# One Strassen step moved from the first output unit to the first b unit, two more places for sums, and a root formed from known parts

## The chip, the cores and the metric

The kernel runs on one core of a Trainium2 chip. The metric is the device time of one execution in microseconds (us). Engines are named as in the profile: PE is TensorE's matmul, PEld its weight load, DVE is VectorE, ACT is ScalarE, POOL is GpSimd, SP is SyncE, which issues most weight loads.

## What is computed

One hybrid decoder block over 256 tokens of width 4096, in float32:

```python
h = rmsnorm(x, norm_w)
proj = h @ w_in                            # 4096 x 20480
u_p, z_p, u_c, b_c, c_c, z_c, g_logit = split(proj)
y_pool = causal_multiscale_pool(u_p, pool_w, pool_scale) * silu(z_p)
y_conv = causal_gated_shortconv(u_c, b_c, c_c, conv_w, conv_b) * silu(z_c)
br = einsum('bsnc,ncd->bsnd', stack([y_pool, y_conv]), w_branch)
gates = sigmoid(g_logit.reshape(b, s, 2, d) + gate_b)
x = x + (sum(gates * br, axis=2) @ w_out)
return rmsnorm(x, final_norm_w)
```

Almost all of the work is the three products with w_in, w_branch and w_out.

## The kernel before

**Units and steps.** The products are cut into units of 1024 output columns, in this order: cz0, cb0, cu0, cc0 (convolution, first half), cz1 to cc1, pz0 to pu1 (pool), g0_0 to g1_0 (gates), b0_0, b1_0, ... b1_3 (branches), o0 to o3 (output). A unit over 4096 rows has 16 steps of 256 rows, a branch unit 8. float32 is kept by splitting each operand into a rounded high part and a rest, so every product takes three matmuls. A step is of one of two kinds, given by a letter of the unit's string (lines 38 to 51): P, plain, with 24 matmuls of 128x512, or S, one Strassen step, with 21. The strings' names count the S steps: NINE_A is cb0's, SEVEN4 is o0's, TEN that of cu0 and of the other units with ten.

**What a step asks of the engines.** SP loads the four weight blocks of a step into `raw` (three and a corner); for an S step POOL adds the third block onto the corner with an accumulating DMA (`gather`). ACT rounds them into the ring (`highs`), DVE subtracts to get the rests (`lows`). For an S step DVE also forms three block sums in `parts`, which ACT rounds and DVE splits again (`rest`, line 308). The ring has 26 cells of 128x512: a P step takes 8, an S step 14, and a cell comes free when PE has used it. So the preparation runs one or two steps ahead of PE, never further. All engines run their queues in program order.

**Stationary operands.** They stand in `arena` as high parts and rests. An S operand has, beside its four blocks, four sums of them (Q3, Q5, Q6, Q7, `sums_s`). There is room for eight S operands; a unit with nine or ten uses operands 6 and 7 as well, whose sums share one tile, `side`: `side_items` (line 553) makes them during cb0 and stores both to DRAM (`aside`, on POOL), and later units load the one they need.

**Ticks.** After every six matmuls one entry of a queue is run (`tick`): epilogues are lists of such entries, with None as a pause. `pop_fill` runs beside them: a `Fill` brings one operand of the branch and output units from DRAM, in phases. It is fetched into a stage (three of them: half of `sa`, and `sb`, `sc`); from 8 ticks on, phase 0 forms the four sums on DVE, phase 1 rounds on ACT 4 ticks later, phase 2 makes the rest on DVE. The sums had one place, `sa[:, 0:4]`, so only one S fill could be between its phases 0 and 2 (line 824). The operands of o0's last steps come from the last branch unit, so they are filled while o0 runs.

**The start and the end.** WARM matmuls on zeros run before the first weights land (line 922). In o3 the last three steps are run per token block, the second one also per half; `finish_half` adds a half and squares it, and `finish` forms 1 / sqrt(mean + eps) with one Newton step (`rstd_of`, line 925), scales the four column blocks and stores them.

Of the kernel before, what the change touches and what calls it, by code (L numbers as in the profile page):

```python
# [9 lines left out]
F32 = mybir.dt.float32  # L10
# [5 lines left out]
P = 128  # L16
# [16 lines left out]
WARM = 18  # L33
# [6 lines left out]
NINE_A = "PSPSSPSPSSPSPSPS"  # L40
NINE_P = "PSPSSPSPSSPSSPSP"
HOST = "PPBPPMMPSSSPSSSPSSS"
SEVEN4 = "PPPPSPSPSPSPSSPS"
# [11 lines left out]
def hybrid_block(ctx: ExitStack, tc: tile.TileContext, x, xc, prm, rows_in, w_in, pool_w, w_branch, w_out, out):  # L55
# [5 lines left out]
    def act(dst, src, func=AF.Copy, **kw):  # L61
        return pin(nc.scalar.activation(dst, src, func, **kw))  # L62
# [22 lines left out]
    def move(dst, src):  # L85
        return pin(nc.scalar.dma_start(dst, src))
# [48 lines left out]
    def norm_col(j):  # L135
        return par[:, j:j + 1]
# [391 lines left out]
    def seq_x(text):  # L528
        if text is FIRST:
            return [("P", i) for i in FIRST]  # L530
        text = [c for c in text if c in "PS"]
        ns = text.count("S")
        if ns > NS + NB:
            ss = list(range(ND, 16)) + [resident[0]]
            if ns > NS + NB + 1:
                resident[0] = 2 * ND - 3 - resident[0]
                ss = [ss[-1]] + ss[:-1] + [resident[0]]
            ps = [i for i in range(ND) if i not in ss]
            return [(c, (ss if c == "S" else ps).pop(0)) for c in text]
        return sequence(text, ND, ND + NS + NB, NB)  # L540
# [12 lines left out]
    def side_items(i):  # L553
        def scaled():
            for k in range(2):
                v = sa[:, 6 - 2 * k:8 - 2 * k]
                act(v, v, scale=norm_col(2 * i + k))

        return [lambda: move(sa[:, 4:].rearrange("p o c -> p (o c)"), xc[i])] + gap(7) + [scaled, None, lambda: sums_s(sa)] + gap(3) + [
            lambda: act(side["tile"][:, 0], sa[:, 0:4]), None,  # L560
            lambda: sub(side["tile"][:, 1], sa[:, 0:4], side["tile"][:, 0].bitcast(F32)),
            None, None, None, None, lambda: aside(side_d[i - ND + 2], side["tile"])]
# [10 lines left out]
    def conv_units(c, first):  # L573
# [39 lines left out]
        u = in_unit(f"cz{c}", base + 3 * HALF, lambda u: silu_y(u.late) + (gap(4) + side_items(ND - 1) + side_items(ND - 2) if first else []),  # L613
                    FIRST if first else EIGHT4, dst=Y)
        u.late = not first
        in_unit(f"cb{c}", base + HALF, b_epi, TEN if c else NINE_A).late = True
# [157 lines left out]
    def out_unit(c):  # L774
# [15 lines left out]
        text = (SEVEN4, NINE, NINE, OUT3)[c]  # L790
# [19 lines left out]
    class Fill:  # L810
        def __init__(self, o, src, free, ready):
            self.o, self.free, self.ready, self.src = o, free, ready, src
            self.at = self.st = None
            self.phase = self.due = 0

# [4 lines left out]
        def advance(self, force):  # L820
            o, q = self.o, self.st
            n = o.n - 4 if o.kind == "S" else 0
            four = sa[:, 0:4]
            if self.phase == 0 and n and any(f.phase and f.o.kind == "S" for f in fills):
                return False
# [26 lines left out]
    stages = [sa[:, 4:8]]  # L852
# [315 lines left out]
    for u in units:  # L1168
        if u.name == "b0_0":
            last_pair["stack"].close()  # L1170
            open_last(F32)
        if u is names["o1"]:
            assert not fills
            more.close()
# [13 lines left out]
        if u is last_x:  # L1188
            side["stack"].close()
            more = ExitStack()  # L1190
            ctx.enter_context(more)
            pool = more.enter_context(tc.tile_pool(name="more", bufs=1))
            apart["tile"] = pool.tile([P, 8 * P], F32R, name="apart")
            stages.extend(pool.tile([P, 4, P], F32, name=name) for name in ("sb", "sc"))
            queue_fills()
# [54 lines left out]

    def finish(t):
        r = rout[:, t:t + 1]
        rstd_of(ossq[:, t:t + 1], r, f"rout{t}")
# [9 lines left out]
    for t in range(2):  # L1263
        for ns in ((0, 1),) if t == 0 else ((0,), (1,)):
# [6 lines left out]
            for n in ns:  # L1271
                finish_half(t, n)
        finish(t)
# [40 lines left out]
```

## Time and profile before

| | us |
|---|---|
| median of 3 runs | 2348.76 (2348.66 to 2349.11) |
| the profiled execution | 2348.53 |
| its span in the trace | 2346.8 |
| PE busy | 2332.0 (99%) |
| DVE busy | 2134.0 (91%) |
| ACT busy | 1539.8 (66%) |

The span runs from the first instruction to the last event; the execution takes 1.7 us more. Busy times overlap between engines. A wait in the trace is idle time of an engine just before an instruction, put down to whatever released it last.

### The profile page before, as it was taken

How to read it: one execution, taken by the hardware profiler on the slowest of the kernel's cores; microseconds unless marked ns; L12 is line 12 of the kernel's file. 1: busy time of each engine (PE TensorE's matmuls, PEld its weight loads, DVE VectorE, ACT ScalarE, POOL GpSimd, SP SyncE). 2: the span in 40 equal slices, each digit the busy share in tenths (PEclk: the TensorE clock that was granted, in tenths of full speed). 3: DMA queues.
4: the chain of work that ended last, by engine and by line, in shares of the span. 5: the costliest groups of instructions: out<-in, count | busy, mean ns of one | idle time of the engine just before them, and what ended most of it. 6: DMA issues, size and time to landing. Idle time of an engine off the chain costs nothing.

```text
span 2346.8 us, 29867 instructions
## 1 busy us (share of the span) xinstructions
PE 2332.0 (99%) x10382; PEld 1930.1 (82%) x10382; DVE 2134.0 (91%) x2177; ACT 1539.8 (66%) x1926; POOL 298.7 (13%) x362
## 2 busy tenths in 40 slices
PE   9999999999999999999999999999999999999998
PEld 7888888888888888888888888888888888878886
DVE  8789999999989979979999899998999889999898
ACT  6666656666666656667766766666676667666664
POOL 0111101111101101101121111111011010011110
PEclk9999999999999999999999999999999999999999
DMA  9789978989978868868999999999889889889998
GB/s 376 247 250 291 273 229 248 282 246 284 271 219 256 264 201 252 257 205 255 290 275 276 307 284 284 278 309 288 277 271 279 273 266 295 272 237 303 290 268 288
DMA packets 203975, 634.60 MB, mean 270 GB/s; under 512 B 21424, under 2 KB 29872, under 8 KB 201008
## 3 DMA queue, kind: packets, MB, share of 16 engines
q1 hardware_dynamic: 134912, 485.42, 59.0%
q0 software_dynamic: 51264, 105.40, 24.7%
q10 hardware_dynamic: 17648, 41.87, 4.9%
q8 instruction: 81, 1.33, 0.2%
q14 instruction: 70, 0.57, 0.1%
HBM read 585.42 MB, written 25.17 MB: 260 GB/s over the span
## 4 chain that ended last, share of the span: by engine, by line
PE 95%; DVE 3%; ACT 1%; issue 1%; DMA 0%; DVEq 0%; SPq 0%; ACTq 0%
PE sums L1096 67%; PE shared L1096 26%; DVE ring L65 2%; PE shared L705 1%; PE shared L483 1%; DVE parts L65 1%; DVE E L65 0%; ACT ring L62 0%; DVE Y L77 0%; DMA raw<-in_w_in_dram 0%; ACT J L62 0%; DVE raw L1259 0%; PE shared L681 0%; ACT Y L62 0%; PE shared L682 0%
## 5 line engine op out<-in xcount | busy, mean ns | idle before, releaser
L1096 PE MATMUL sums<-ring,arena 128*128 128x512 f32 x6732 | 1611.3, 390 | 2.9 <-ACT arena L62 1.3
L1096 PEld LDWEIGHTS sums<-ring,arena 128*128 128x128 f32 x6732 | 1262.2, 188 | 267.2 <-DVE ring L65 2.9
L65 DVE TENSOR_TENSOR ring<-raw,ring 128x512 fp32r<-128x512 f32 (+2 forms) x979 | 1091.8, 1140 | 143.9 <-PE sums L1096 57.5
L62 ACT ACTIVATE ring<-raw 128x512 fp32r<-128x512 f32 (+1 forms) x942 | 899.3, 1015 | 89.6 <-PE sums L1096 65.0
L62 ACT ACTIVATE ring<-parts 128x1024 fp32r<-128x1024 f32 (+1 forms) x493 | 399.7, 823 | 542.8 <-DVE parts L65 487.7
L1096 PE MATMUL shared<-ring,arena 128*128 128x512 f32 x2319 | 590.1, 389 | 0.0
L1096 PEld LDWEIGHTS shared<-ring,arena 128*128 128x128 f32 x2319 | 435.3, 188 | 90.3
L65 DVE TENSOR_TENSOR ring<-parts,ring 128x1536 fp32r<-128x1536 f32 (+2 forms) x274 | 416.7, 1533 | 4.8 <-ACT ring L62 4.6
L92 POOL DMA_DIRECT2D raw<-in_w_in_dram x178 | 153.9, 864 | 1369.2 <-DMA raw<-in_w_in_dram 518.1
L65 DVE TENSOR_TENSOR parts<-raw,parts 128x1024 f32<-128x1024 f32 x236 | 288.5, 1222 | 0.0
L65 DVE TENSOR_TENSOR parts<-raw 128x512 f32<-128x512 f32 x236 | 162.9, 690 | 2.2
L65 DVE TENSOR_TENSOR J<-J 128x512 f32<-128x512 f32 (+1 forms) x90 | 78.3, 870 | 15.1 <-ACT J L62 12.5
L62 ACT ACTIVATE E<-sums 128x512 f32<-128x512 f32 x76 | 42.1, 596 | 47.1 <-PE sums L1096 46.1
L62 ACT ACTIVATE J<-shared 128x512 f32<-128x512 f32 x128 | 68.3, 620 | 6.6 <-PE shared L1096 6.4
L1096 PE MATMUL sums<-ring,last_pair 128*128 128x512 f32 x261 | 66.1, 389 | 0.0
L1096 PE MATMUL shared<-ring,side 128*128 128x512 f32 x261 | 66.0, 389 | 0.0
L1096 PE MATMUL shared<-ring,last_pair 128*128 128x512 f32 x252 | 63.6, 389 | 0.0
L92 POOL DMA_DIRECT2D raw<-in_w_out_dram x33 | 28.7, 870 | 273.8 <-DVE ring L65 142.5
L92 POOL DMA_DIRECT2D raw<-in_w_branch_dram x25 | 21.7, 869 | 287.7 <-DVE ring L65 69.0
L1096 PEld LDWEIGHTS shared<-ring,side 128*128 128x128 f32 x261 | 49.0, 188 | 10.2
L1096 PEld LDWEIGHTS sums<-ring,last_pair 128*128 128x128 f32 x261 | 49.0, 188 | 10.2
L1096 PEld LDWEIGHTS shared<-ring,last_pair 128*128 128x128 f32 x252 | 47.3, 188 | 9.8
(133 smaller groups left out, 729.6 us busy)
## 6 DMA issues: line engine op xcount, KB each, us to landing
raw<-in_w_in_dram SPq DMA_DIRECT2D x318, 768.0 KB, 6.9
raw<-in_w_in_dram SPq DMA_DIRECT2D x326, 256.0 KB, 6.0
raw<-in_w_branch_dram SPq DMA_DIRECT2D x64, 768.0 KB, 7.2
raw<-in_w_out_dram SPq DMA_DIRECT2D x64, 768.0 KB, 7.1
raw<-in_w_in_dram POOLq DMA_DIRECT2D x178, 256.0 KB, 6.7
raw<-in_w_branch_dram SPq DMA_DIRECT2D x64, 256.0 KB, 5.6
raw<-in_w_out_dram SPq DMA_DIRECT2D x64, 256.0 KB, 6.0
E<-J POOLq DMA_DIRECT2D x30, 512.0 KB, 10.3
```

The source lines that it names most:

```text
L62: return pin(nc.scalar.activation(dst, src, func, **kw))
L65: return pin(nc.vector.tensor_tensor(out=dst, in0=a, in1=b, op=op))
L92: return pin(nc.gpsimd.dma_start(dst, src, accum_op=ALU.add))
L483: pin(nc.tensor.transpose(shared(j)[:, i * T + t * P:i * T + (t + 1) * P], src[:, t, c:c + P], ident))
L705: pin(nc.tensor.matmul(o, a, b, start=(k, i) == (0, 0), stop=(k, i) == (3, 2)))
L1096: pin(nc.tensor.matmul(ps, lhs, rhs, start=n == 0, stop=n == u.total[b] - 1))
```

## The change

Five parts: cb0 gets ten S steps (TEN_B), the sixth of them with operand 7 and the last with operand 6; `side_items` makes the two sides one behind the other, and writes the second into the tile once the step with the first is behind it in the program. o0 gets six S steps (SIX5). From b1_3 on, the memory of `apart` (an operand of the b0 units) is taken by two more places for sums, `sd` and `se`. The root at the end is formed from the sum of what is known (`partial`) and the last sum of squares. WARM goes from 18 to 23.

```diff
-WARM = 18
+WARM = 23
-NINE_A = "PSPSSPSPSSPSPSPS"
+TEN_B = ("PSPSSPSSP", "SSPSSPS")
-SEVEN4 = "PPPPSPSPSPSPSSPS"
+SIX5 = "PPPPPSPSPSPSPSPS"
...
     def seq_x(text):
+        if text is TEN_B:
+            ss = list(range(ND, 13)) + [ND - 1] + list(range(13, 16)) + [ND - 2]
+            ps = list(range(ND - 2))
+            return [(c, (ss if c == "S" else ps).pop(0)) for c in "".join(text)]
...
-        return [lambda: move(sa[:, 4:].rearrange("p o c -> p (o c)"), xc[i])] + gap(7) + [scaled, None, lambda: sums_s(sa)] + gap(3) + [
-            lambda: act(side["tile"][:, 0], sa[:, 0:4]), None,
-            lambda: sub(side["tile"][:, 1], sa[:, 0:4], side["tile"][:, 0].bitcast(F32)),
-            None, None, None, None, lambda: aside(side_d[i - ND + 2], side["tile"])]
+            def high():
+                st = next(s for s in steps[16:] if s.op is x_ops[a] and s.kind == "S")
+                assert i == a or state["now"] > steps.index(st)
+                act(side["tile"][:, 0], sa[:, 0:4])
+
+            return [scaled, None, lambda: sums_s(sa)] + gap(3) + [
+                high, None, lambda: sub(side["tile"][:, 1], sa[:, 0:4], side["tile"][:, 0].bitcast(F32))]
+
+        def keep(i):
+            return lambda: aside(side_d[i - ND + 2], side["tile"])
+
+        return [fetch(a)] + gap(7) + made(a) + [fetch(b)] + gap(3) + [keep(a)] + gap(3) + made(b) + gap(4) + [keep(b)]
...
-            four = sa[:, 0:4]
-            if self.phase == 0 and n and any(f.phase and f.o.kind == "S" for f in fills):
-                return False
+            if self.phase == 0 and n:
+                used = [f.four for f in fills if f.phase and f.o.kind == "S"]
+                self.four = next((q for q in fours if not any(q is u for u in used)), None)
+                if self.four is None:
+                    return False
+            four = self.four
...
+        if u is names["b1_3"]:
+            lone.close()
+            lone = ExitStack()
+            ctx.enter_context(lone)
+            pool = lone.enter_context(tc.tile_pool(name="lone", bufs=1))
+            fours.extend(pool.tile([P, 4, P], F32, name=name) for name in ("sd", "se"))
...
+    known = sb("known", [P, 2, 4])
+
+    def partial(t):
+        b, h = known[:, t, 0:1], known[:, t, 1:2]
+        pin(nc.vector.tensor_reduce(out=b, in_=ossq[:, t, 0:4], axis=mybir.AxisListType.X, op=ALU.add))
+        pin(nc.vector.tensor_scalar(out=b, in0=b, scalar1=1.0 / D, scalar2=EPS, op0=ALU.mult, op1=ALU.add))
+        pin(nc.vector.tensor_scalar(out=h, in0=b, scalar1=-0.5, scalar2=None, op0=ALU.mult))
+
     def finish(t):
         r = rout[:, t:t + 1]
-        rstd_of(ossq[:, t:t + 1], r, f"rout{t}")
+        b, h, q, s = (known[:, t, i:i + 1] for i in range(4))
+        act(s, ossq[:, t, 4:5], AF.Sqrt, scale=1.0 / D, bias=b)
+        stt(h, ossq[:, t, 4:5], -0.5 / D, h, ALU.mult, ALU.add)
+        pin(nc.vector.reciprocal(out=r, in_=s))
+        stt(q, r, h, r, ALU.mult, ALU.mult)
+        stt(r, q, 1.5, r, ALU.add, ALU.mult)
...
             for n in ns:
                 finish_half(t, n)
+            if 0 in ns:
+                partial(t)
```

What moves in the engines' queues is shown at three places. First DVE in the second half of o0, where fills' sums and rests stand between the steps' preparations; `ring` and `parts` belong to steps, `sa`, `sb`, `sc`, `sd` and `arena` to fills. Before:

```order
L65 TENSOR_TENSOR arena<-sa,arena 128x512
L65 TENSOR_TENSOR arena<-sb,arena 128x384
L65 TENSOR_TENSOR sa<-sa 128x128 x4
L65 TENSOR_TENSOR ring<-raw,ring 128x1024
L65 TENSOR_TENSOR ring<-raw,ring 128x512 x2
L65 TENSOR_TENSOR parts<-raw 128x512
```

Now:

```order
L65 TENSOR_TENSOR sa<-sa 128x128 x4
L65 TENSOR_TENSOR sd<-sb 128x128
L65 TENSOR_TENSOR sd<-sd,sb 128x128
L65 TENSOR_TENSOR sd<-sb 128x128
L65 TENSOR_TENSOR sd<-sb,sd 128x128
L65 TENSOR_TENSOR ring<-raw,ring 128x1536
L65 TENSOR_TENSOR ring<-raw,ring 128x512
L65 TENSOR_TENSOR arena<-sa,arena 128x512 x2
```

Before, a fill's sums came behind the rest of the fill ahead of it; now the sums of two fills follow one another, the second in `sd`. In the rest of o0 `sd` is not used again, and `se` nowhere.

Second DVE at the end of o0: the sums of the last fill, the preparation of a P and of an S step, and the last fill's rest (the two rows that write `arena`). Before:

```order
L65 TENSOR_TENSOR sa<-sb,sa 128x128
L65 TENSOR_TENSOR ring<-raw,ring 128x1536
L65 TENSOR_TENSOR ring<-raw,ring 128x512
L65 TENSOR_TENSOR parts<-raw 128x512
L65 TENSOR_TENSOR ring<-raw,ring 128x512
L65 TENSOR_TENSOR parts<-raw,parts 128x1024
L65 TENSOR_TENSOR ring<-raw,ring 128x1536
L65 TENSOR_TENSOR ring<-parts,ring 128x1536
L65 TENSOR_TENSOR arena<-sa,arena 128x512
L65 TENSOR_TENSOR arena<-sb,arena 128x512
```

Now:

```order
L65 TENSOR_TENSOR sa<-sa 128x128 x4
L65 TENSOR_TENSOR ring<-raw,ring 128x1536
L65 TENSOR_TENSOR ring<-raw,ring 128x512
L65 TENSOR_TENSOR parts<-raw 128x512
L65 TENSOR_TENSOR ring<-raw,ring 128x512
L65 TENSOR_TENSOR parts<-raw,parts 128x1024
L65 TENSOR_TENSOR ring<-raw,ring 128x1536
L65 TENSOR_TENSOR ring<-parts,ring 128x1536
L65 TENSOR_TENSOR arena<-sa,arena 128x512
L65 TENSOR_TENSOR arena<-sa,arena 128x384
```

Here nothing moved: another operand is filled last, at the same place among the steps.

Third DVE behind the first token block's scaling, in the last part of o3. `sums_84` and `sums_85` are the PSUM banks of the second token block's halves, `J` holds the half times the final weight. Before:

```order
L65 TENSOR_TENSOR E<-sums_84,E 128x512
L65 TENSOR_TENSOR J<-E,Y 128x512
L65 TENSOR_TENSOR E<-sums_85,E 128x512
L65 TENSOR_TENSOR J<-E,Y 128x512
L929 TENSOR_REDUCE rout_m<-ossq 128x1
L930 TENSOR_SCALAR rout_m<-rout_m 128x1
L932 RECIPROCAL rout<-rout_s 128x1
L65 TENSOR_TENSOR rout_m<-rout_m,rout 128x1
L77 SCALAR_TENSOR_TENSOR rout_m<-rout_m,rout 128x1
L77 SCALAR_TENSOR_TENSOR rout<-rout_m,rout 128x1
```

Now:

```order
L65 TENSOR_TENSOR E<-sums_84,E 128x512
L65 TENSOR_TENSOR J<-E,Y 128x512
L1284 TENSOR_REDUCE known<-ossq 128x1
L1285 TENSOR_SCALAR known<-known 128x1
L1286 TENSOR_SCALAR known<-known 128x1
L65 TENSOR_TENSOR E<-sums_85,E 128x512
L65 TENSOR_TENSOR J<-E,Y 128x512
L77 SCALAR_TENSOR_TENSOR known<-ossq,known 128x1
L1293 RECIPROCAL rout<-known 128x1
L77 SCALAR_TENSOR_TENSOR known<-rout,known 128x1
L77 SCALAR_TENSOR_TENSOR rout<-known,rout 128x1
```

Three instructions moved from behind the last half's add to ahead of it, and one product is gone.

More of the change, by code (lines that the diff above doesn't have):

```diff
@@ L551, in side_load, with side_items, fetch, made @@
         aside(side["tile"], side_d[i - ND + 2])
[L553 to L557, printed above, removed]
-        return [lambda: move(sa[:, 4:].rearrange("p o c -> p (o c)"), xc[i])] + gap(7) + [scaled, None, lambda: sums_s(sa)] + gap(3) + [
-            lambda: act(side["tile"][:, 0], sa[:, 0:4]), None,
-            lambda: sub(side["tile"][:, 1], sa[:, 0:4], side["tile"][:, 0].bitcast(F32)),
-            None, None, None, None, lambda: aside(side_d[i - ND + 2], side["tile"])]
+    def side_items(a, b):
+        def fetch(i):
+            return lambda: move(sa[:, 4:].rearrange("p o c -> p (o c)"), xc[i])
+        def made(i):
+            def scaled():
+                for k in range(2):
+                    v = sa[:, 6 - 2 * k:8 - 2 * k]
+                    act(v, v, scale=norm_col(2 * i + k))
+            def high():
[7 more added lines that the diff above has]
+        return [fetch(a)] + gap(7) + made(a) + [fetch(b)] + gap(3) + [keep(a)] + gap(3) + made(b) + gap(4) + [keep(b)]
     def silu_y(late):
@@ L611, in c_epi @@
             return items + gap(5) + [lambda: put(y_d[1, c], chan(E))]
-        u = in_unit(f"cz{c}", base + 3 * HALF, lambda u: silu_y(u.late) + (gap(4) + side_items(ND - 1) + side_items(ND - 2) if first else []),
+        u = in_unit(f"cz{c}", base + 3 * HALF, lambda u: silu_y(u.late) + (gap(4) + side_items(ND - 1, ND - 2) if first else []),
                     FIRST if first else EIGHT4, dst=Y)
         u.late = not first
-        in_unit(f"cb{c}", base + HALF, b_epi, TEN if c else NINE_A).late = True
+        in_unit(f"cb{c}", base + HALF, b_epi, TEN if c else TEN_B).late = True
         u = in_unit(f"cu{c}", base, lambda u: rescale(Y), TEN, dst=Y)
@@ L788, in epi @@
                 lambda: mul(E, E, Y[:, 0:1].to_broadcast([P, 2, NU]))] + gap(4) + [lambda: move(o_d[c], E)]
-        text = (SEVEN4, NINE, NINE, OUT3)[c]
+        text = (SIX5, NINE, NINE, OUT3)[c]
         u = Unit(f"o{c}", lambda i: w_out[c, i], seq_x(text), m_ops, epi, before=start if c == 3 else None)
@@ L814, in __init__ @@
             self.phase = self.due = 0
+            self.four = None
         def fetch(self, st):
@@ L850, in advance @@
             return True
-    stages = [sa[:, 4:8]]
+    stages, fours = [sa[:, 4:8]], [sa[:, 0:4]]
     fills = deque()
@@ L1171, in hybrid_block @@
             open_last(F32)
+        if u is names["b1_3"]:
[4 more added lines that the diff above has]
+            fours.extend(pool.tile([P, 4, P], F32, name=name) for name in ("sd", "se"))
         if u is names["o1"]:
             assert not fills
+            lone.close()
             more.close()
@@ L1192, in hybrid_block @@
             pool = more.enter_context(tc.tile_pool(name="more", bufs=1))
-            apart["tile"] = pool.tile([P, 8 * P], F32R, name="apart")
             stages.extend(pool.tile([P, 4, P], F32, name=name) for name in ("sb", "sc"))
+            lone = ExitStack()
+            ctx.enter_context(lone)
+            apart["tile"] = lone.enter_context(tc.tile_pool(name="lone", bufs=1)).tile([P, 8 * P], F32R, name="apart")
             queue_fills()
```

## Prediction

> **What bounds the kernel now.** I read the engines' shares of the span first, on the page:
>
> ```profile
> PE 2332.0 (99%) x10382; PEld 1930.1 (82%) x10382; DVE 2134.0 (91%) x2177; ACT 1539.8 (66%) x1926; POOL 298.7 (13%) x362
> ```
>
> TensorE (PE) is busy for 2332.0 of 2346.8 us. A change can therefore win in three ways only: fewer matmuls, the few microseconds in which PE stands, and the ends of the span. Next, what PE waited for, in the view of waits for PE alone (total us, times, longest):
>
> ```profile
> PE sums L1096 <- ACT arena L62: 1.3, 1, 1.3
> PE shared L923 <- DVE warm L919: 1.1, 1, 1.1
> ```
>
> The second stands before the warming matmuls. The first, 1.3 us on ScalarE (ACT) writing the arena, is one wait in o0, at 2087 us. The price of a matmul comes from the chain of work (start, us, what): one P step, 24 matmuls.
>
> ```profile
> 256.06 5.44 PE sums L1096 x24
> ```
>
> That is 5.44 / 24 = 0.2267 us each, so a P step takes 5.44 us of PE and an S step, 21 matmuls, 4.76 us. What a step asks of VectorE (DVE) stands in the groups kept apart by shape (count | busy us, mean ns):
>
> ```profile
> L65 DVE TENSOR_TENSOR ring<-raw,ring 128x1536 fp32r<-128x1536 f32 x379 | 665.0, 1755 | 44.4 <-ACT ring L62 24.4 <-issue 15.5 <-DMA raw<-in_w_in_dram 2.3
> L65 DVE TENSOR_TENSOR ring<-raw,ring 128x512 fp32r<-128x512 f32 x529 | 361.6, 690 | 92.8 <-PE sums L1096 56.6 <-PE shared L1096 29.5 <-ACT J L62 2.7
> L65 DVE TENSOR_TENSOR ring<-parts,ring 128x1536 fp32r<-128x1536 f32 x198 | 347.5, 1755 | 3.8 <-ACT ring L62 3.6
> L65 DVE TENSOR_TENSOR parts<-raw,parts 128x1024 f32<-128x1024 f32 x236 | 288.5, 1222 | 0.0
> L65 DVE TENSOR_TENSOR parts<-raw 128x512 f32<-128x512 f32 x236 | 162.9, 690 | 2.2
> ```
>
> A P step takes the first two rows, 1.755 + 0.690 = 2.45 us. An S step takes all five, 6.11 us. So S trades 0.68 us of PE for 3.67 us of DVE, and pays only where DVE has room. The windows of three units show the room (length, then busy us of PE, PEld, DVE, ACT, POOL; granted clock, DMA share, GB/s):
>
> ```profile
> 94.70:175.70 81.00, 81.00 (x359) 67.05 (x358) 69.81 (x72) 55.26 (x69) 8.86 (x11) 1.00 0.85 254
> 175.70:255.90 80.20, 80.20 (x356) 66.40 (x355) 76.20 (x73) 51.45 (x64) 11.73 (x13) 1.00 0.92 279
> 2006.40:2092.40 86.00, 84.65 (x380) 69.64 (x379) 81.35 (x101) 56.66 (x77) 6.91 (x8) 1.00 0.85 253
> ```
>
> These are cb0 (nine S), cu0 (ten S) and o0 (seven S). In cb0 and cu0 PE never stops, though cu0 keeps DVE at 95%. In o0 PE stands 1.35 us.
>
> **The first b unit, nine S to ten.** PE loses 24 - 21 = 3 matmuls: -0.68 us. DVE gets 3.67 us more: 69.81 + 3.67 = 73.5 of 80.3 us, below the 76.20 of 80.20 that cu0 carries without a stop, in the same order of P and S. So the step is hidden and the 0.68 us are won. The tenth S step needs the pair kept on the side to be used twice: first the rows of one pair, which GpSimd stores to DRAM, then those of the other in the same place. ACT may write the second over the first only after that store has been read out. The view of these tiles, and two rows of POOL's timeline:
>
> ```profile
> L62 ACT ACTIVATE side<-sa x2: 612/615/618, 127.2 to 158.0; 128x512 fp32r<-128x512 f32 x2
> ...
> DMA to landing us min/median/max: 6.3/8.2/11.0
> 136.95 0.66 POOL L89 DMA_DIRECT2D side_d<-side  x1
> 147.96 0.85 POOL L92 DMA_DIRECT2D raw<-in_w_in_dram  x1 [10.36 <-DMA raw<-in_w_in_dram]
> ```
>
> Before, the store is issued at 136.95 us and the second write comes at 158.0. The new list puts that write 10 ticks instead of 15 behind the store's place; a tick is six matmuls, 1.36 us, so it moves 6.8 us forward, to 151.2. The store stands behind the same gather on POOL as before, but the place into which that gather goes is now freed by a P step, which reads its corner last, where an S step reads it first. I estimate that at up to 3 us, so the issue at 137 to 140 and the landing, with 6.3 to 11.0 us, at 143 to 151. Likeliest: no wait. Queued behind ACT's write would be the roundings for the ring, and behind them DVE and PE. Bounds: 0 and some 4 us, for one gather more ahead of the store (the next one comes 147.96 - 136.95 = 11 us later; the spare time and the ring's lead of some 2 us go off). I take 0.
>
> **o0, seven S to six.** PE gains 3 matmuls: +0.68 us. The two swaps cancel. What counts is the stall, in the timeline and, in the last row, a window:
>
> ```profile
> 2080.28 5.60 PE L1096 MATMUL sums<-ring,last_pair 128*128 128x512 f32 x24
> ...
> 2085.97 0.61 ACT L62 ACTIVATE arena<-sa 128x512 fp32r<-128x512 f32 x1
> 2086.49 0.61 ACT L62 ACTIVATE arena<-sb 128x512 fp32r<-128x512 f32 x1
> ...
> 2087.16 1.30 PE L1096 MATMUL sums<-ring,arena 128*128 128x512 f32 x3 [1.27 <-ACT arena L62]
> 2087.23 0.68 DVE L65 TENSOR_TENSOR arena<-sb,arena 128x512 fp32r<-128x512 f32 x1
> ...
> 2087.96 0.30 PEld L1096 LDWEIGHTS sums<-ring,arena 128*128 128x128 f32 x2 [0.51 <-DVE arena L65]
> 2051.00:2087.00 36.00, 34.89 (x154) 28.55 (x153) 35.22 (x50) 23.45 (x30) 3.44 (x4) 1.00 0.81 237
> ```
>
> The last step of o0 waits for its own operand, filled last: rounded by ACT until 2087.10, its rest made by DVE until 2087.91. The P step ahead of it runs from 2080.28, so its successor was due at 2080.28 + 5.44 = 2085.72. It comes at 2087.16, 1.44 us late, and then loses 0.5 us to DVE: **1.9 us** in all. ACT came late because its work ahead waited on DVE, which is busy for 35.22 of the 36 us from 2051 to 2087.
>
> The order at the end of o0 shows the last fill at the same place as before: behind one whole S preparation and ahead of the first evacuation. So the change does not call it earlier. What helps is the backlog ahead of it: one S fewer in o0 takes 3.67 us from DVE, PE gives 0.68 us more time, and no two S steps stand next to each other. Moved forward by 3.67 us, ACT's two writes would end at 2087.10 - 3.67 = 2083.4 and DVE's rest at 2084.2, against a need at 2085.7 + 0.68 = 2086.4. The program can't issue them before the P step's first six matmuls, 2080.28 + 0.68 + 1.36 = 2082.3, plus 1.1 + 0.7 us of work: 2084.1. Some 2 us are spare either way. The two new places for sums add nothing to DVE's work (same four sums a fill); they let one fill's sums be formed while another is being rounded, once in this stretch. Bounds: -1.9 us (all of the stall) and 0 (the last fill is fetched no earlier, and the backlog comes back). I take **-1.9**, since 2 us spare is more than half of the 3.67 us.
>
> **The start.** Five more warming matmuls. A window, and the timeline behind it:
>
> ```profile
> 6.02:9.36 3.34, 3.34 (x8) 2.66 (x9) 2.29 (x5) 2.00 (x4) 0.00 (x0) 1.00 1.02 321
> ...
> 15.33 2.01 ACT L62 ACTIVATE ring<-raw 128x1536 fp32r<-128x1536 f32 x2 [1.78 <-DMA raw<-in_w_in_dram]
> ...
> 18.67 0.30 PEld L1096 LDWEIGHTS sums<-ring,arena 128*128 128x128 f32 x2 [0.16 <-DVE ring L65]
> ```
>
> The first 8 real matmuls take 3.34 / 8 = 0.42 us each against 0.2267 later, while the granted clock's column says 1.00. Without the slow ones PE would be 8 x 0.2 = 1.6 us ahead by 9.36. It can't keep that: at 18.67 it already waits 0.16 us for DVE's split, which takes what ACT rounded from 15.33 on, after 1.78 us of waiting for a weight load; the DMA engines' share is 1.02 in the window. None of these waits for PE. So the gain ends there: **-0.1**, between +0.2 (a warming matmul in the way) and -0.6 (the spread of the runs shown, 2348.53 to 2349.11, if it is the start's). Beside these rows: the Trainium skill, "TensorE: Matmul & The Clock Gate", Part 1, says that full speed comes after one busy window of about 3.4 us, and that the windows run freely. The trace agrees: the slow rate ends 3.34 us after PE's pause. By that rule alone, with the pause filled, the sum would be 1.5 us lower; the wait at 18.67 speaks against it.
>
> **The end.** For the second token block (timeline):
>
> ```profile
> 2335.98 0.18 ACT L62 ACTIVATION_READ_ACCUMULATOR sa<-E 128x1 f32 x1
> 2336.05 0.68 DVE L65 TENSOR_TENSOR E<-sums,E 128x512 f32<-128x512 f32 x1
> ...
> 2337.53 0.16 DVE L929 TENSOR_REDUCE rout_m<-ossq 128x1 f32<-128x5 f32 x1
> 2337.72 0.15 DVE L930 TENSOR_SCALAR rout_m<-rout_m 128x1 f32<-128x1 f32 x1
> ...
> 2338.92 1.15 ACT L62 ACTIVATE raw<-raw,rout 128x1024 f32<-128x1024 f32 x1 [0.81 <-DVE rout L77]
> ```
>
> From the last add to the scaling 2338.92 - 2336.05 = 2.87 us pass. The new root leaves out the reduce, one tensor_scalar and one product behind the last sum of squares, 0.19 us apart each: -0.58. But its three preparing instructions stand on DVE ahead of that last add, and the first needs the sum of squares of the half before, read out at 2336.16. So the add starts at 2336.16 + 0.03 + 3 x 0.19 = 2336.8 instead of 2336.05. The same saving for the first token block brings DVE 0.05 to 0.2 us earlier. Net: -0.58 + 0.72 - 0.05 to 0.2, between -0.1 and +0.1: **0.0**.
>
> **Sum.** The profiled execution took 2348.53 us (span 2346.8 plus 1.7 around it): 2348.53 - 0.68 + 0.68 - 1.9 - 0.1 + 0.0 = 2346.5. The median is 2348.76, 0.23 above it; I put half of that back: **2346.6**.
>
> **Rivals.**
> 1. The stall in o0 stays, whole or in part, since the last fill's place is the same: 2346.6 + 0.9 to 2346.6 + 1.9, so 2347.5 to 2348.5. For it: the same order. Against: DVE's 3.67 us.
> 2. Slower: ACT waits in cb0 for the side store. It decides when the store lands after about 151 us by this trace, that is with one more gather ahead of it. Price 2 to 6 us on ACT, of which PE loses up to 4 after the ring's lead: 2346.6 + 2.3 to 4 = 2348.9 to 2350.6, and more if the units after it, cu0 at 95% of DVE first, start without a lead.
> 3. The start's 1.5 us survive, or the small waits between cb0 and o0 shrink, since every epilogue from cu0 on moves by half a tick (three matmuls):
>
> ```profile
> PEld sums L1096 <- DVE ring L65: 2.9, 7, 0.7
> ```
>
> Either gives 2346.6 - 1.5 = 2345.1; those waits can as well grow by as much, which with the forecast's gain is 2348.1.
>
> **How the numbers follow.** Forecast 2346.6 (2346.0 to 2347.4): 60%. Rival 1: 18%. Rival 2: 9%. Rival 3: 10% below (3% the start by the rule on the clock, 7% the small waits), 3% above. A change of 0.2%, 4.7 us, is about what a measurement of this kernel can tell from no change. Faster than 2344.1 would need all of the forecast, the start and the small waits together: 4%. Slower than 2353.5 needs twice rival 2's price: 4%. The rest, 92%, is within. The range takes in the forecast, rival 1, the upper side of rival 3 and the near edges of the rest, some 83% in all: 2345.2 to 2349.0.
>
> **What would show it.** Right: no wait of PE for ACT arena at the end of o0; cb0 as long as cu0 (80.2 us) with PE never idle; ACT's second write of the side near 151 without a wait; the first step's matmuls at 0.23 us, and the same wait of PE for DVE near 18.7; the last add some 0.5 to 0.7 us after PE's last matmul, and 2.3 us from it to the scaling. Wrong: PE idle in cb0 behind ACT, PE waiting for the arena again, or a longer wait in cz1 or pz0.

## The result: slower by a quarter of a percent

| | us | executions |
|---|---|---|
| before, on the same chip | 2349.31 (2348.66 to 2350.61) | 10 |
| the changed kernel | 2355.03 (2354.0 to 2357.99) | 10 |
| ratio | 1.0026, 95% interval 1.0016 to 1.0036 | |
| the changed kernel's profiled execution | 2357.99 (span 2356.2) | |

The forecast was 2346.6, with a range up to 2349.0. The changed kernel is 5.7 us slower instead of 2.2 us faster. Its profiled execution is the slowest of its ten, 3 us above the median, and the text says below where these 3 us lie.

The parts that the prediction asked about first. Three stretches of the changed kernel (windows: bounds, length, busy time of PE, PEld, DVE, ACT and POOL with counts, granted clock, DMA share, GB/s): the first 3.4 us of real matmuls, then o0, then cb0.

```profile
5.90:9.30 3.40, 3.26 (x13) 2.33 (x14) 2.54 (x6) 2.44 (x5) 0.00 (x0) 1.00 1.02 319
...
2016.20:2101.20 85.00, 85.00 (x384) 70.27 (x383) 77.79 (x99) 54.95 (x75) 6.87 (x8) 1.00 0.83 254
95.00:175.40 80.40, 80.40 (x355) 66.44 (x354) 72.74 (x76) 56.67 (x72) 9.64 (x12) 1.00 0.87 258
```

All three came in kind as predicted: 13 matmuls stand in the first window where 8 stood before, cb0 takes 80.4 us instead of 80.9 with PE never idle, and in o0, 85.0 us instead of 86.0, PE is busy throughout: the wait for the arena at its end is gone. Then PE's matmuls in the timeline of the opening, and the second token block at the end:

```profile
5.96 11.78 PE L1116 MATMUL sums<-ring,arena 128*128 128x512 f32 x49 [0.64 <-DVE ring L818]
18.74 1.42 PE L1116 MATMUL sums<-ring,arena 128*128 128x512 f32 x5 [1.01 <-DVE ring L65]
```

```profile
2334.77 10.59 PE L1116 MATMUL sums<-ring,arena 128*128 128x512 f32 x46
...
2345.60 0.15 DVE L1286 TENSOR_SCALAR known<-known 128x1 f32<-128x1 f32 x1
2345.67 0.68 DVE L65 TENSOR_TENSOR E<-sums,E 128x512 f32<-128x512 f32 x1
...
2348.11 1.15 ACT L62 ACTIVATE raw<-raw,rout 128x1024 f32<-128x1024 f32 x1 [0.68 <-DVE rout L77]
```

The time won by the warm clock is spent in a wait of 1.01 us at 18.74, as forecast. At the end the last add starts 0.31 us after PE's last matmul (2334.77 + 10.59 = 2345.36), behind the last preparing instruction, and the scaling follows it by 2.44 us; 0.5 to 0.7 and 2.3 were expected.

So the loss is elsewhere. The groups by form (count, busy us, mean ns) show one of its places. The changed kernel, then the kernel before:

```profile
L1116 PE MATMUL sums<-ring,last_pair 128*128 128x512 f32 x261 | 67.9, 395 | 0.0
L1116 PE MATMUL shared<-ring,last_pair 128*128 128x512 f32 x252 | 65.6, 397 | 0.0
```

```profile
L1096 PE MATMUL sums<-ring,last_pair 128*128 128x512 f32 x261 | 66.1, 389 | 0.0
L1096 PE MATMUL shared<-ring,last_pair 128*128 128x512 f32 x252 | 63.6, 389 | 0.0
```

The same 513 matmuls, those that take their weights from the tile `last_pair`, last 6 to 8 ns longer; no other group of matmuls of 512 columns moved by more than 1 ns. From start to start they take 234.0 ns instead of 226.7 in the mean, which makes 513 x 7.3 ns = 3.7 us. Nobody waits for anybody in these rows. What the change did to `last_pair` is an address: the small tiles of its side of the memory take 32 bytes each, the new root has one of them (`known`) where the old one had four, and everything below moved up by 96 bytes: `last_pair` from 166912, a multiple of 512, to 167008.

The waits of PE show the other place: before, then the changed kernel.

```profile
PE sums L1096 <- ACT arena L62: 1.3, 1, 1.3
...
PE sums L1096 <- DVE ring L65: 0.6, 2, 0.3
```

```profile
PE sums L1116 <- DVE ring L65: 5.5, 5, 1.8
...
PE sums L1116 <- ACT ring L62: 0.2, 1, 0.2
```

A wait of 1.3 us for the arena is gone, and waits of 4.9 us for DVE's rests have come. The timeline finds the two longest at the end of b0_1 and at the start of b1_3. First b0_1 (ACTq and SPq are DMA issues; the bracket is the idle time before the instruction and who ended it):

```profile
1780.89 0.70 ACTq L86 DMA_DIRECT2D m_d<-last_pair  x1
...
1794.98 0.32 ACTq L86 DMA_DIRECT2D sa<-m_d  x1
1795.35 0.63 ACT L62 ACTIVATE ring<-parts 128x512 fp32r<-128x512 f32 x1 [4.09 <-DMA m_d<-last_pair]
...
1796.97 1.76 DVE L65 TENSOR_TENSOR ring<-parts,ring 128x1536 fp32r<-128x1536 f32 x1 [2.74 <-ACT ring L62]
...
1798.78 0.73 PE L1116 MATMUL sums<-ring,arena 128*128 128x512 f32 x2 [1.29 <-DVE ring L65]
```

ACT's queue issues the fetch of a fill from `m_d`, and this fetch waits until the store of `m_d`, issued at 1780.89, has landed 14.1 us later. Behind it stands ACT's rounding for the next Strassen step, behind that DVE, behind DVE PE. PE's clock falls as well: for 3.41 us from 1799.66 on the granted clock is 0.50, and 10 matmuls are counted there; 17 are counted in the next 3.41 us, at 1.00. Then b1_3:

```profile
1972.85 0.66 ACT L62 ACTIVATE arena<-sb 128x512 fp32r<-128x512 f32 x1
1973.37 1.60 ACT L62 ACTIVATE J<-shared 128x512 f32<-128x512 f32 x3
1973.54 0.69 DVE L65 TENSOR_TENSOR arena<-sb,arena 128x512 fp32r<-128x512 f32 x1 [3.67 <-ACT arena L62]
1974.15 0.68 DVE L65 TENSOR_TENSOR parts<-raw 128x512 f32<-128x512 f32 x1
...
1980.89 1.43 PE L1116 MATMUL sums<-ring,arena 128*128 128x512 f32 x5 [1.79 <-DVE ring L65]
```

A fill's rounding (`arena<-sb`) stands between ACT's evacuations at the start of b1_3; DVE's rest of that fill waits 3.67 us for it, and behind the rest stands the first Strassen step of b1_3.

Unit lengths, from a unit's first matmul to the next unit's, tell the profiles apart best (found by counting 24 matmuls for a plain and 21 for a Strassen step in the trace). A typical unit with one Strassen step on `last_pair` is cu0.

| us | cb0 | cu0 | cz1 | pz0 | b0_1 | b1_3 | o0 |
|---|---|---|---|---|---|---|---|
| before | 80.9 | 80.2 | 85.8 | 85.9 | 42.6 | 41.6 | 86.0 |
| changed | 80.4 | 80.4 | 86.7 | 86.5 | 46.3 | 43.6 | 85.0 |

### The profile page after: what moved, and what is told of

It is laid out like the page before. It is cut to its first block, busy times and chain, and to the rows that moved or that the text cites. A ratio compares the mean times of both kernels' runs of the same rounds, so it can differ in the third digit from the quotient of the medians.

```text
span 2356.2 us, 29862 instructions
## 1 busy us (share of the span) xinstructions
PE 2337.7 (99%) x10387; PEld 1930.2 (82%) x10387; DVE 2133.7 (91%) x2166; ACT 1542.6 (65%) x1918; POOL 295.0 (13%) x362
## 4 chain that ended last, share of the span: by engine, by line
PE 95%; DVE 2%; DMA 1%; ACT 1%; issue 0%; SPq 0%; ACTq 0%; DVEq 0%
PE sums L1116 67%; PE shared L1116 27%; PE shared L721 1%; DVE ring L65 1%; PE shared L483 1%; DMA m_d<-last_pair 1%; DMA raw<-in_w_in_dram 1%; DVE E L65 0%; ACT ring L62 0%; DVE parts L65 0%; DVE Y L77 0%; DVE J L65 0%; DVE raw L1301 0%; PE shared L697 0%; ACT E L62 0%
## 5 line engine op out<-in xcount | busy, mean ns | idle before, releaser
L62 ACT ACTIVATE ring<-raw 128x1536 fp32r<-128x1536 f32 (+2 forms) x936 | 900.1, 1022 | 99.8 <-PE sums L1116 66.7
L1116 PEld LDWEIGHTS sums<-ring,last_pair 128*128 128x128 f32 x261 | 49.1, 188 | 12.1
```

What stands on the lines that cost most here:

```text
L1116: pin(nc.tensor.matmul(ps, lhs, rhs, start=n == 0, stop=n == u.total[b] - 1))
```

## Experiments

Sixteen kernels ran, timed in turns with the kernel before: 10 or 11 executions of each (4 of e11), 27 or 33 of before. e1 to e4 ran on one chip, e5 to e12 on a second and e13 to e16 on a third. Each result stands beside the median of before from its own turns, since these medians differ by half a microsecond. Steps of one microsecond between medians are smaller than the intervals of the ratios, so where one rests on less than 2 us the unit lengths of the traces carry it.

### The address of the weights

```diff
-    sb("back", [P, 40])
+    sb("back", [P, 64])      # e1, the changed kernel: 96 bytes more
+    sb("back", [P, 16])      # e2, the kernel before: 96 bytes less
+    sb("back", [P, 24])      # e3, the kernel before: 64 bytes less
```

> The changed kernel with 96 bytes of padding beside its small tiles, so that last_pair and every tile above it stand at the same SBUF addresses as before the change (last_pair back from 167008 to 166912); no instruction is added or moved. Theory A (the matmuls whose weights come from last_pair are slower because of the tile's address): the start-to-start time of those 513 matmuls goes from 234.0 ns back to 226.7 ns, their mean duration from 395 and 397 ns to 389, and the time falls by 513 x 7.3 ns = 3.7 us, to about 2351.3 us. Rival R1 (they are slower because other work moved beside them, the address means nothing): 397 ns as before, time 2355.0.

> The kernel of before with 96 bytes less of padding, so that its tiles stand at the changed kernel's addresses (last_pair at 167008); nothing else. Theory A: the matmuls on last_pair take 395 to 397 ns instead of 389 and the time rises by 3.7 us, from 2349.3 to 2353.0 us, with the same waits as before. Rival R1: no difference, 2349.3.

> The kernel of before with 64 bytes less, last_pair at 166976, a multiple of 64 but not of 128. Theory A1 (what counts is that the address is no multiple of 64): 389 ns and 2349.3 us, no difference. Theory A2 (any departure from a multiple of 128 or more costs): as with 96 bytes, about 396 ns and 2353.0 us. R1: 2349.3 with 389 ns.

Measured: e1 2350.14 us (before 2349.15; ratio 1.0004, 0.9995 to 1.0013), e2 2353.89 (ratio 1.0020, 1.0011 to 1.0028), e3 2352.72 (1.0016, 1.0007 to 1.0024). Groups by form of e1, then of e2:

```profile
L1116 PE MATMUL sums<-ring,last_pair 128*128 128x512 f32 x261 | 66.2, 389 | 0.0
L1116 PE MATMUL shared<-ring,last_pair 128*128 128x512 f32 x252 | 63.6, 389 | 0.0
```

```profile
L1096 PE MATMUL sums<-ring,last_pair 128*128 128x512 f32 x261 | 67.9, 395 | 0.0
L1096 PE MATMUL shared<-ring,last_pair 128*128 128x512 f32 x252 | 65.6, 397 | 0.0
```

Padding alone takes the changed kernel's matmuls back to 389 ns, and the lack of 96 bytes alone gives the kernel before its 395 and 397. Theory A holds, in both directions; R1 falls. The price is larger than the estimate: 4.9 us off the changed kernel, 4.7 us onto the kernel before, where 3.7 stood. From start to start the matmuls on the arena account for the missing one: 226.88 ns in the changed kernel against 226.75 in the one before and 226.77 in e1, some 9000 times. In the changed kernel and in e2, 0.8 us of it stand in the twelve matmuls behind each stretch of matmuls on `last_pair`. And 64 bytes are no safe raster: e3 has 233.4 ns, against A1.

Three more kernels asked what it is about the address: other tiles moved and `last_pair` not (e10), the arena moved down by 64 bytes and nothing else (e11), `last_pair` moved by 128 (e12), all on the kernel before.

```diff
-    sb("back", [P, 40])
+    sb("back", [P, 16])      # e10, with [P, 24] of padding above last_pair in its own pool
+    sb("back", [P, 8])       # e12
-    blocks("front", [P, 96])
+    blocks("front", [P, 80]) # e11, with [P, 16] of padding between arena and ring
```

> The kernel of before with raw, parts, sa, Y and the small tiles 96 bytes higher, as in the changed kernel, but last_pair at its old address 166912. Theory A (the weights' address alone costs): matmuls on last_pair 226.7 ns from start to start, 389 ns long, time 2349.3 us, within 1 us. Rival R7 (part of the 4.7 us comes from ACT, DVE or DMAs at tiles off the 64-byte raster): 2350 to 2354 us, with matmuls on the arena at 226.9 ns as in the kernel with 96 bytes less.

> The kernel of before with the arena, where nine tenths of the stationary operands stand, 64 bytes lower (2496 instead of 2560); every other large tile at its old address. Theory A: as with last_pair at a 64-byte offset (233.4 ns instead of 226.7), all of its 9051 matmuls slow down, 9051 x 6.8 ns = 61 us: about 2410 us, those on last_pair, side and extra stay at 226.7 ns. Rival R8 (something particular to last_pair's place, next to the streams into raw, makes the loss): less than 5 us.

> The kernel of before with last_pair 128 bytes higher, at 167040, a multiple of 128 but not of 256 or 512. Theory A3 (what counts is the place of the 512 bytes that one weight row takes from a partition, 128 columns of 4 bytes, against a raster of 512): slow as with 64 and 96 bytes, 233 to 234 ns, 2352.7 to 2353.9 us. Theory A4 (a raster of 128 bytes): 226.7 ns and 2349.3 us.

Measured: e10 2349.41 us (before 2349.42; ratio 0.9999, 0.9990 to 1.0008), e11 2367.69 (1.0078, 1.0064 to 1.0092), e12 2353.54 (1.0018, 1.0009 to 1.0028). The arena's groups in e11, which stood at 390 and 389 ns before:

```profile
L1097 PE MATMUL sums<-ring,arena 128*128 128x512 f32 x6732 | 1626.3, 392 | 1.9 <-ACT arena L62 1.2 <-DVE ring L803 0.6
L1097 PE MATMUL shared<-ring,arena 128*128 128x512 f32 x2319 | 595.3, 392 | 0.0
L1097 PE MATMUL sums<-ring,last_pair 128*128 128x512 f32 x261 | 66.2, 389 | 0.0
```

Of the tiles that moved, only the one with the weights matters: `raw`, `parts`, `sa`, `Y` and the small ones, moved by 96 bytes, cost nothing (e10, R7 falls, and with it the extra microsecond as a cost of other engines). It isn't particular to `last_pair` (e11 loses 18.3 us, R8 falls), and 128 bytes aren't a safe raster either (A4 falls). But the estimate of 61 us for e11 missed: a matmul on the arena took 228.9 ns from start to start, 2.2 more than in its old place and a third of what `last_pair` loses in e3. The two offsets are not the same, either: the arena stood 64 bytes below a multiple of 512, `last_pair` 64 above. Why the amount differs stays open.

### The half tick, and the order of the fills

With the address out of the way 3.0 to 3.2 us are missing between e1 (0.8 to 1.0 above before) and the forecast (2.2 below). In e1's trace cz1 takes 86.5 us, pz0 86.3 and b1_3 43.6: 0.6 + 0.5 + 2.0 = 3.1 more than before.

```diff
         combine(u)
+        if u.name in ("cb0", "o0"):
+            state["mm"] += 3                 # e4, on e1
```

> The padded changed kernel, in which three matmuls are added to the tick count at the end of cb0 and of o0, so that all entries of the queue from cu0 on come at the same matmul of each unit as before the change (cb0 and o0 keep their new strings). Theory H (the new stalls of 1 to 4 us at b0_1 and at b1_3 come from the half tick by which ten Strassen steps in cb0 shift everything behind them): the waits at the end of b0_1 and at the start of b1_3 are gone as before the change, and the time is 2 to 4 us below the padded kernel, 2347 to 2349 us. Rival R2 (they come from the places for sums sd and se or from the order of the memories of apart, sb and sc, or by chance from run to run): same as the padded kernel, 2351.3, with both waits there.

Measured: 2348.57 us (2347.15 to 2353.68; before 2349.15). cz1 and pz0 are back at 85.9 and 85.7 us: those two waits were the half tick. But b1_3 takes 42.7 us, only 0.9 less (o0 takes 84.8, 0.2 less), and the profiled execution, the slowest, has the wait in b0_1 at its largest (48.6 us). The rows of cz1 show how: DVE and PE's wait in the changed kernel, then in e4.

```profile
384.09 0.68 DVE L65 TENSOR_TENSOR E<-J,Y 128x512 f32<-128x512 f32 x1
...
384.69 0.68 DVE L65 TENSOR_TENSOR parts<-raw 128x512 f32<-128x512 f32 x1
...
388.83 0.98 PE L1116 MATMUL sums<-ring,arena 128*128 128x512 f32 x3 [0.75 <-DVE ring L65]
```

```profile
382.54 0.69 DVE L65 TENSOR_TENSOR parts<-raw 128x512 f32<-128x512 f32 x1
...
384.88 0.69 DVE L65 TENSOR_TENSOR E<-J,Y 128x512 f32<-128x512 f32 x1
...
387.29 1.43 PE L1116 MATMUL sums<-ring,arena 128*128 128x512 f32 x5 [0.25 <-DVE ring L65]
```

In the changed kernel, shifted by half a tick, an epilogue's product (`E<-J,Y`, 0.68 us) stands ahead of the forming of a step's `parts`; in e4 it stands behind, and PE's wait shrinks by half a microsecond. So H holds for cz1, pz0 and about half of b1_3's wait, and falls for b0_1 and for the other half.

The fills are queued in the order in which o0 uses its operands, and SIX5 has a fifth P ahead of the first S; the next two kernels put that to the test.

```diff
-SEVEN4 = "PPPPSPSPSPSPSSPS"
+SEVEN4 = "PPPPPSPSPSPSPSPS"   # e5, the kernel before: the new string alone
-SIX5 = "PPPPPSPSPSPSPSPS"
+SIX5 = "PPPPSPPSPSPSPSPS"     # e6, on e4
```

> The kernel of before with o0's string alone replaced by the six-step one (no new places for sums, all else and all addresses as before). Fills are queued in the order in which o0 uses its operands; the new string has a fifth plain step ahead of the first Strassen step, so that the fill of plain operand 4 is fetched before that of the first Strassen operand and is rounded at the start of b1_3. Theory J (b1_3's new wait comes from this order of the fills): b1_3 is 1.1 to 2 us longer (42.7 to 43.6 us instead of 41.6), o0 1.0 to 1.2 us shorter (84.8 to 85.0 instead of 86.0), time 2349 to 2350 us. Rival R3 (the wait comes from sd and se or the memory under them): b1_3 41.6 us, time 2348.0.

> The changed kernel padded by 96 bytes and with the tick count corrected, and with o0's fifth plain step put behind its first Strassen step (PPPPSPPSPSPSPSPS, still six), so that the fills up to b1_3 come in the order of before. Theory J: b1_3 is back at 41.6 us, o0 stays near 85.0, and the time is 1.1 us under that of the padded kernel with ticks (2348.6): 2347.2 to 2347.6 us, the gain that the prediction had (-1.9 us from before's median). Rival R3: b1_3 at 42.7 us and 2348.6.

Measured: e5 2350.96 us (before 2349.66; ratio 1.0006, 0.9997 to 1.0015) with b1_3 at 42.7, e6 2347.53 (ratio 0.9992, 0.9983 to 1.0000) with b1_3 at 41.6 and o0 at 84.8. J holds: the string alone makes 1.1 us of the wait in b1_3, and the other 0.9 us of the changed kernel's 2.0 is the half tick. Two expectations missed, for one reason: in e5 o0 took 86.0 us and not 85, and the time lies above the 2349 to 2350 expected, since the wait at o0's end stayed. Its row in e5's waits, for DVE's `arena`:

```profile
PE sums L1096 <- DVE arena L65: 1.0, 1, 1.0
```

With 3 matmuls more than before, o0 is as long as before, so of its 1.9 us of stall some 0.6 went and 1.3 stayed. One Strassen step less does not by itself remove that stall. e9, below, follows this up.

### The fetch that waits for a store

```diff
-    LANDING, STORED, QUIET, HUSH, REST = 8, 7, 5, 20, 5
+    LANDING, STORED, QUIET, HUSH, REST = 8, 10, 5, 20, 5    # e8, on e6
...
-                merged[c] = now[0] + STORED
+                merged[c] = now[0] + (10 if c == 0 else STORED)     # e15, on before
```

> The kernel with pad, ticks and order, in which a fill waits 10 ticks instead of 7 after the store of its source was issued before it is fetched. Theory K (the wait of 1 to 5 us at the end of b0_1 in some executions comes from a fetch on ACT's queue that waits for the store of m_d, whose landing varies between 11 and 14 us): no execution has that wait, b0_1 takes 42.6 us, the spread of the executions shrinks to about 1.5 us (from 2347.2 to 2353.7 in the kernel with pad and ticks) and the median falls by 0 to 0.5 us. Rival R5 (something else delays ACT there): spread and wait as before.

> The kernel of before, in which only the fills whose source is the first part of m_d wait 10 ticks instead of 7 after its store. Theory K (that wait also strikes some executions of the kernel of before): b0_1 always 42.6 us, spread about 1 us instead of 3 to 7, median 2348.4 to 2348.8. Rival R5 (it comes with the change alone): 2349.3, spread as before.

Measured: e8 2346.36 us (2346.11 to 2346.84; before 2349.66; ratio 0.9985, 0.9976 to 0.9994), e15 2348.48 (2348.19 to 2349.26; before 2349.11, 2348.13 to 2352.29). ACT's queue in e8:

```profile
1775.68 0.65 ACTq L86 DMA_DIRECT2D m_d<-last_pair  x1
...
1785.94 0.62 ACT L62 ACTIVATE ring<-parts 128x512 fp32r<-128x512 f32 x1
1787.38 1.06 ACT L62 ACTIVATE ring<-parts 128x1024 fp32r<-128x1024 f32 x1 [0.82 <-DVE parts L65]
1790.14 0.32 ACTq L86 DMA_DIRECT2D sa<-m_d  x1
```

The store lands just as late here, 14.4 us after its issue, but the fetch now stands behind the rounding of `parts`, and nothing urgent stands behind the fetch. K holds: the spread falls from 6.5 us (e4) and 3.2 us (e6) to 0.7 us, and b0_1 takes 42.6. The wait belongs to no version. In the traces of e2, e3 and e12, which are the kernel before with other padding, b0_1 takes 43.5, 42.9 and 43.3 us; in e2 the store is issued at 1781.3, lands 12.1 us later, and the fetch goes out at that moment, at 1793.45. Without the wait the kernel before is 0.6 us faster, and its executions lie within 1.1 us instead of 4.2. e8 is the fastest kernel of the study, 3.3 us below before and 8.7 below the changed one.

> The changed kernel with 96 bytes of padding and 10 ticks after a store, but with the shifted ticks and the order of fills that it brought. Theory H+J (those two are what is left between it and the best kernel): cz1 86.5 and pz0 86.3 instead of 85.9 and 85.8, b1_3 42.7 to 43.6 instead of 41.6, time 2346.4 + 1.1 + 1.1 to 2.0 = 2348.6 to 2349.5 us. Rival R10 (with the store's wait gone both are hidden): 2346.4 to 2347.0.

Measured: e16 2353.2 us (2351.55 to 2356.09), far above its expectation. Two things were left out of that. With the half tick uncorrected, the rest of o0's last fill is only made when the step already needs it: PE waits 1.8 us for it, and o0 takes 86.8 us where e8 takes 84.8. That the ten ticks delay it so far is the likely reason, since e1, the same kernel with seven, has o0 at 85.0. And the wait in b1_3, alone, can cost the clock. The same two stretches around it in e16 and in e1, whose b1_3 has the same wait (windows; the column after POOL is the granted clock):

```profile
1971.80:1974.00 2.20, 0.42 (x3) 0.03 (x1) 2.20 (x3) 2.20 (x4) 1.13 (x2) 1.00 0.33 60
1974.00:1977.40 3.40, 3.40 (x9) 2.66 (x10) 3.40 (x3) 0.55 (x1) 1.29 (x2) 0.60 0.87 158
```

```profile
1971.80:1974.00 2.20, 0.42 (x3) 0.01 (x1) 2.20 (x3) 2.20 (x4) 1.11 (x2) 1.00 0.59 114
1974.00:1977.40 3.40, 3.40 (x15) 2.83 (x16) 3.40 (x3) 0.57 (x1) 1.31 (x2) 1.00 0.86 153
```

After the same 2.2 us with three matmuls, e16's next 3.4 us ran at a granted clock of 0.60 with 9 matmuls, e1's at 1.00 with 15: six matmuls of 0.227 us, 1.4 us, lost or not lost. With e8's 2346.36, 1.1 us for cz1 and pz0, 2.0 for b1_3 and 2.1 for o0 the sum is 2351.6, and e16's five fastest executions took 2351.55 to 2352.02; the others lie 1.2 us and more above, as they would where the clock fell, but only the profiled one has a trace. So H and J hold and R10 falls, but its time doesn't measure the two alone.

### The three terms that the prediction had

```diff
-            fours.extend(pool.tile([P, 4, P], F32, name=name) for name in ("sd", "se"))
+            for name in ("sd", "se"):
+                pool.tile([P, 4, P], F32, name=name)     # e9, on e8: one place for sums
-WARM = 23
+WARM = 18                                                # e7 on e6, e13 on e8
-        b, h, q, s = (known[:, t, i:i + 1] for i in range(4))
...
+        rstd_of(ossq[:, t:t + 1], r, f"rout{t}")         # e14, on e8, and no partial
```

> The kernel with pad, ticks, order and 10 ticks after a store, with one place for sums as before the change (sd and se take their memory but are not used); the fill before the last one is then made 8 ticks later, the last one at the same tick. The prediction's theory (o0's wait went because DVE has one Strassen step less in o0; the places add nothing): o0 84.8 us, time 2346.4. Rival R6 (the second place is what moves DVE's work away from the end of o0; six steps without it kept 1.1 us of the wait): o0 85.5 to 86.0 us, time 2347.0 to 2347.6.

> The same with 18 warming matmuls instead of 23. Theory W (the five more only move a wait, since weight loads set the pace of the first steps): cz0 as long as with 23 within 0.3 us, the first eight matmuls at 0.43 us each, time within 0.5 us of the kernel with 23. Rival R4 (the clock's slow start costs its 1.5 us, and the new waits near 17 us have nothing to do with it): 1.5 us slower.

> The kernel with pad, ticks, order and 10 ticks after a store, whose executions lie within 0.7 us, with 18 warming matmuls instead of 23. Theory W (weight loads set the pace of the first steps, the faster first matmuls only wait longer): 2346.4 us within 0.3. Rival R4 (the clock's slow start costs its whole 1.5 us): 2347.9.

> The same kernel (23 warming matmuls) with the root formed as before the change, all large tiles at the same addresses. The prediction's term (the shorter root and the later last add cancel): 2346.4 us within 0.2. Rival R9 (the three preparing instructions fit beside PE's last matmuls, so that the new root gains its 0.3 to 0.5 us): 2346.7 to 2346.9.

Measured: e9 2347.75 us (2346.9 to 2348.54; before 2349.42), o0 85.8 us against e8's 84.8, with a wait of 0.6 us for DVE's `arena` at its end. R6 holds and the prediction's theory falls: the second place is worth about 1 us in o0 between these two traces. The amount is not fixed: e7, which has both places like e6, has o0 at 85.5 us in its trace and 0.4 us of the same wait.

```profile
2085.79 0.50 PE L1116 MATMUL sums<-ring,arena 128*128 128x512 f32 x1
2085.95 0.69 DVE L65 TENSOR_TENSOR arena<-sa,arena 128x512 fp32r<-128x512 f32 x1
```

In e9's timeline the rest of the last fill starts at 2085.95, after the first matmul of the step that needs it; in e6 it starts 1.0 us before that matmul.

e7 2348.3 us (2347.2 to 2352.75) against e6's 2347.53 in the same turns; e13 2346.96 (2346.34 to 2347.47; before 2349.11) against e8's 2346.36 in others. Both differences, 0.8 and 0.6 us, lie between what W and R4 expected. The medians can't tell more: in e7 the store's wait strikes again, and e13 and e8 ran on different chips.

The traces tell more, for they show that 18 warming matmuls do not always start slowly. Of the ten traces with 18, six have eight or more slow matmuls at the start (before, e2, e5, e10, e11, e13), and four have none (e3, e7, e12, e15); so e7's trace missed W's 0.43 us. With 23 none of the eight traces starts so. All twelve that start at full speed then wait 0.8 to 1.3 us for DVE ahead of the 50th matmul, and none of the six others does. cz0 ends 94.7 to 95.5 us after the span's start in the slow ones, 95.1 in the mean (without e11, whose arena moved), and at 94.3 to 95.5, 94.9 in the mean, in the twelve. So the trade that W describes is there, R4's 1.5 us are not, and what is left, 0.2 us, is less than the scatter.

e14 2346.56 us (2345.89 to 2347.27) against e8's 2346.36. The last add comes at 2333.97 in e14 and the scaling 2.87 us behind it, in e8 at 2334.10 and 2.45 us; counted from the first matmul of o3 the scaling comes at 84.7 us in both. The term of 0.0 holds.

## Why the prediction was wrong

**The step that failed first is one that isn't in it: what the root's edit does to the memory.** The part on the end counts the root's instructions, 0.58 us less against 0.72 more, and puts its tiles at nothing, without a reason. Four tiles of 32 bytes became one, and 513 weight loads left their place at a multiple of 512: 4.7 us to 4.9 us (e2, e1), two and a half times the largest gain in the sum. No engine waits longer by it, so no view of waits could have shown it; only the addresses of the two programs would. None of the three rivals named it either.

**The second is rival 3's last sentence, mis-sized.** It saw that every epilogue from cu0 on moves by half a tick, and gave the small waits 1.5 us either way, with 3% for the upper side. Between e1 and e4 lie 0.6 us in cz1, 0.6 in pz0, 0.9 in b1_3 and 0.2 in o0: 2.3 us, all on the upper side.

**The third is the reading of o0's string.** The prediction counted its matmuls and DVE's work, and took its fills to stand at the same place. The last one does. But the string also orders the fills, and the fifth plain operand came one unit earlier, into b1_3: 1.1 us (e5 against before, e6 against e4).

From the forecast of 2346.6 to the 2355.03 measured are 8.4 us. The address with 4.9 us (e1), the half tick with 2.3 and the fills with 1.1 make 8.3. They come from medians and traces of different turns, and what the store's wait adds to the changed kernel's median is not shown, so that they meet so closely is in part luck.

**The terms that it had were right in size.** cb0: -0.68 forecast, -0.7 measured with the address restored (80.2 us in e1, e4 and e6, where before takes 80.9); rival 2, ACT waiting for the side store, didn't come. The tile `side` in the changed kernel:

```profile
L62 ACT ACTIVATE side<-sa x2: 617/617/617, 131.0 to 154.6; 128x512 fp32r<-128x512 f32 x2
```

ACT's second write of it is at 154.6, not near 151, but the first, at 131.0, is 3.8 us later than before too, and no ACT row is among those who waited for this tile. o0: -1.9 + 0.68 = -1.2 forecast, -1.2 measured (84.8 us) once the half tick is restored, -1.0 in the changed kernel itself. The start: the mechanism was right, the new wait stands where it was expected, and the -0.1 taken can't be told from the 0.2 us of the traces or from nothing. The end: 0.0 forecast, 0.2 us at most measured.

**Right for a wrong reason: o0's stall.** The prediction put all of it down to DVE's 3.67 us of saved work and wrote that the two places add nothing. With the string alone 1.3 us of 1.9 stay (e5), and without the places 1.0 us come back (e9). So its "2 us spare" were not there: in these traces the step saved brings less than half, and the second place, put at nothing, the rest. That the sum of the two came to the whole stall was luck.

Put together, e8 and e15, both without the store's wait, stand 2346.36 to 2348.48: a gain of 2.1 us for the five parts, as forecast (2.2), once address, half tick and fill order are as before the change. The two ran on different chips; e14, which is e8 with the old root and ran in e15's turns, stands 1.9 us below it. That e8 waits ten ticks for all parts of `m_d` and e15 for the first alone is a difference that was not tried out.

The profiled execution of the changed kernel is 3 us above its median, and its b0_1, 46.3 us, is 3.7 us longer than in e1. Of these, 1.5 us are PE's waits behind the store's landing, and 1.6 are the seven matmuls by which the lower clock fell short. That the other nine had less of both fits, but they have no trace.

## What to carry to other kernels

An edit that adds or drops even the smallest tile moves every tile that is stacked below it: compare the addresses of all stationary operands before and after, and keep them where they were (here: multiples of 512 bytes; 256 was not tried). Where a string or a count feeds a scheduler, follow all that is derived from it, the order of prefetches and the remainder of a tick count too, up to the end of the program, not just the edited place. And a fetch that depends on a store belongs behind the urgent work of its queue, with room for the store's latest landing: here it came after 8.6 us in one trace and after 14.4 in another.

## What the runs showed of the hardware

The speed of these matmuls depends on the address of their weights. 128x128 float32 weights take 512 bytes of a partition; means from start to start of the 128x512 matmul (other types and shapes, and the address of the moving operand, were not tried):

| weights' address, modulo 512 | ns | run |
|---|---|---|
| 0 | 226.7 | before, e1 |
| 64 | 233.4 | e3 |
| 96 | 234.0 | e2, changed |
| 128 | 232.2 | e12 |
| 448 (the arena) | 228.9 | e11 |

The single values repeat: at 64 they alternate between 231 and 236, at 96 and 128 they come back every seventh matmul, within a nanosecond or two. The weight load's own row stays at 188 ns in every run, so the profile's duration of a load doesn't show it; the matmul's does. The Trainium skill, "SBUF — State Buffer", section "Operand start alignment", asks only that an operand starts at a multiple of its element size, and says that this is about legality, not speed; these runs add the speed.

A wait of PE of 1.8 us can be followed by 3.4 us at a lower clock, or not, with the same wait in the same place (e16 and e1 above). In e16 the granted clock is 0.50 for 3.41 us from 1974.65 on; in the changed kernel it is so for 3.41 us behind a wait of 1.3 us in b0_1, in e4 for 6.83 us around two waits of 1.4 and 1.3 us there. The Trainium skill, "TensorE: Matmul & The Clock Gate", Part 1, lets the clock fall after at least one idle window of about 3.4 us; in e16 it fell after a stretch of 2.2 us in which PE still had three matmuls. By that rule it would have held, and the measurement decides: a wait well under a window was enough in three of these executions, and not in e1's. What decides between them stays open.

The store of 512 KB to `m_d` landed 8.6 us after its issue in the profile of before, 11.7 in e1 and 14.1 to 14.4 in the changed kernel and e8. A fetch that waits for it holds up all that stands behind it in ACT's queue: 4.09 us in the changed kernel.
